# Decay tables and rotary tables moved into the ring of result tiles, seven prepared weights in both layers, and a planner fed with other durations

## The chip, the cores and the metric

One core of a Trainium2 chip runs the whole program. The metric is the device time of one execution in microseconds (us); the profile is of one further execution. TensorE is PE in the profile, VectorE DVE, ScalarE ACT, GpSimd POOL, SyncE SP.

## The reference

Two requests (`x_prompt`, `x_sample`; 512 rows of 1024 each) go through the same two layers and a last RMSNorm, all in float32:

```
layer 1:  x += DiffAttention(RMSNorm(x))   q, k: 16 half-heads of 128; v: 8 heads of 256; rotary on q and k;
          p = softmax(q k'), a = p[first half-head] - lam * p[second]; o = a v; RMSNorm per head;
          o * silu(gate) @ w_out
layer 2:  x += BidirRetention(RMSNorm(x))  q, k: 8 heads of 128 with another rotation; v: 8 heads of 256;
          forward and backward retention with decay exp(-|i-j| * exp(decay)) per head and direction;
          RMSNorm per head; o * silu(gate) @ w_out
y = RMSNorm(x) * final_norm_g
```

Each layer has one input projection (1024 to 8192 columns in layer 1, 1024 to 6144 in layer 2: q, k, v and gate) and one output projection (2048 to 1024).

## The kernel before, in words

**Arithmetic.** Every float32 operand is split in a rounded high part and the rest (`hi_of`, a cast on ACT, L462; `lo_of`, a subtraction on DVE, L465), and each product is three matmuls on these parts (`PASSES`). The two projections also use a seven-product scheme (Strassen's kind): seven products P1 to P7 in place of eight, over the two halves of the columns and of the depth, at the price of sums of weights (`combine`, DVE, L601) and of results (`sums`, DVE, L714).

**A unit** is 256 columns of an input projection. A "pair" unit (q, k, gate) multiplies with the weights stationary: one product is 12 matmuls of 128x512 (`pair_product`, L637). A "wide" unit (v) has 4 times 12 matmuls of 128x256 per product (L685). For a product `prep` loads the raw weights (512 KB each, ring `raw` of 4), sums them where needed (ring `st` of 3) and splits them into the ring `ws` of prepared weights. A pair product takes one place of `ws`, a wide one two. `projections` prepares ahead as far as the ring holds: `WS_BUFS = [7, 6]`, seven places in the second layer (first number), six in the first. The seventh place of layer 1, `ws6`, holds the second request's scaled rotary tables (`ts`, L1026) instead.

**Results** leave the PSUM banks as copies (ring `c`, ACT, L706) and as sums in the ring `e` of eight tiles of 512 columns (`e_t`). For q and k `rot_done` turns them by the tables and `store` splits them into a tile of the ring `os` (three tiles of 1024 columns) and writes that to HBM with two DMAs (`qk<-os`). For v `v_done` splits straight into `os` and writes (`v<-os`). For the gate `gate_done` works in place in the `e` tile and writes that tile (`g<-e`). A place of a ring is free when the last user of its former tile is done, a DMA out of it included: of a q or k unit's four `os` tiles the fourth takes the place of the first, and waits for the first one's store to land.

**Decay tables.** `decay_table(h)` makes, once per head and between the units of the second projection, a 128x896 table of decay factors: it loads distances from HBM (`dist_in`, 448 KB) into one `os` tile, computes the middle 128 columns on DVE (L1487, L1489, L1491), takes three exponentials on ACT (L1492, L1494, L1496) and writes the table to HBM (`f_d[h]`). The retention stage reads it back.

**The stages** by the profile's time: start 0 to 45 us, first input projection to 640, attention with the output projection of layer 1 woven in to 1045, second input projection to 1500, retention with the output projection of layer 2 to the end.

**What sets the order.** All engines are in program order, written out ahead of the run by `Plan`. Each call of `pe`, `act`, `dve`, `pool`, `dma` records one operation with its engine, an assumed duration (`pe(2.79, ...)`, or for ACT and DVE a base and a slope times the number of elements passed, as in `dve(S, ...)` with S = 512), and the tiles that it reads and writes. `arrange` then takes, engine by engine, the ready operation that is due first, counting from these assumed durations, and `issue` keeps the best of three such arrangements. So a changed duration or ring changes the order on all engines, even where no instruction is added. SP has one queue: a DMA that waits for its data or its place holds all DMAs behind it.

## Time and profile before

| | |
|---|---|
| three runs | 1833.98, 1838.55, 1843.78 us (median 1838.55) |
| the profiled execution | 1848.99 us, its span on the core 1847.2 us |
| PE busy | 1796.4 us, 97% of the span, 10100 matmuls |
| DVE, ACT, POOL busy | 1480.1, 1034.9, 227.9 us |
| DMA | 393.85 MB, mean 213 GB/s |

PE counts as busy from a matmul's start to its modelled end, and matmuls overlap; what is not busy, 50.8 us, is time in which PE had nothing in work. In a table of stages each row has the stage, its length, the busy time of each engine with the number of instructions, the granted PE clock (1.00 is full) and the DMA share. In a list of waits each row names who waited for whom, then the total in us, the times, and the longest. In a chain each row is the start, the length and what ran.

### The profile page before, as it was taken

Reading aid. Unit: us, or ns where it says so; the run is one execution under the profiler, and the core shown is the slowest. Engines: PE = TensorE matmul, PEld = TensorE weight load, DVE = VectorE, ACT = ScalarE, POOL = GpSimd, SP = SyncE. Lnnn points to the kernel's source line nnn. Section 1 sums busy time; section 2 is a strip of 40 time slices with the busy share of each in tenths; the row PEclk is TensorE's granted clock in tenths of the full one; section 3 lists DMA queues with packets and bytes.
Section 4 is the critical chain, followed back from the end, with each engine's and each line's share of the span. In section 5 each row is a group of like instructions: output and inputs, shape, how many; then the busy total and the mean of one; then the engine's idle time right before and its main releaser. Section 6 shows DMA issues by size and latency. Waiting matters only on the chain.

```text
span 1847.2 us, 28202 instructions
## 1 busy us (share of the span) xinstructions
PE 1796.4 (97%) x10100; PEld 1545.2 (84%) x10100; DVE 1480.1 (80%) x2597; ACT 1034.9 (56%) x2154; POOL 227.9 (12%) x372
## 2 busy tenths in 40 slices
PE   7999999999999999999999999999999999999997
PEld 6987988988988878888888788978888897888876
DVE  8988778778777998888888898686767758777677
ACT  7644434344434587777777774444443547666663
POOL 2000000000000033333333100000000000111111
PEclk9999999999999999999999999999999999999999
DMA  7557956975544678888785467787784568989883
GB/s 264 194 151 218 264 170 193 269 214 157 172 143 137 230 263 254 250 228 244 231 248 180 138 197 205 229 240 203 216 234 143 165 227 295 248 241 263 235 242 137
DMA packets 195116, 393.85 MB, mean 213 GB/s; under 512 B 16032, under 2 KB 75040, under 8 KB 194848
## 3 DMA queue, kind: packets, MB, share of 16 engines
q1 hardware_dynamic: 172160, 350.02, 56.3%
q0 software_dynamic: 22528, 41.95, 14.5%
q8 instruction: 79, 1.29, 0.3%
q14 instruction: 61, 0.50, 0.1%
q10 hardware_dynamic: 288, 0.08, 0.0%
HBM read 254.10 MB, written 175.64 MB: 233 GB/s over the span
## 4 chain that ended last, share of the span: by engine, by line
PE 74%; DMA 9%; DVE 8%; ACT 4%; issue 3%; POOL 1%; SPq 0%; DVEq 0%; POOLq 0%; ACTq 0%
PE bank L637 34%; PE bank L685 16%; PE bank L1373 10%; PE bank L1564 4%; PE bank L1256 3%; PE bank L1205 3%; DMA b<-w1P 2%; DMA qk<-os 2%; PE bank L1546 2%; DVE b L465 1%; PE bank L893 1%; DMA raw<-in_da_w_in_dram 1%; PE bank L1241 1%; DMA b<-in_da_w_out_dram 1%; DMA b<-w0P 1%
## 5 line engine op out<-in xcount | busy, mean ns | idle before, releaser
L637 PE MATMUL bank<-arena,ws 128*128 128x512 f32 x2202 | 529.2, 394 | 14.1 <-ACT ws L462 7.2
L637 PEld LDWEIGHTS bank<-arena,ws 128*128 128x128 f32 x2202 | 413.8, 189 | 107.0 <-ACT c L706 9.4
L637 PE MATMUL bank<-b,ws 128*128 128x512 f32 x1170 | 287.9, 393 | 2.8 <-DVE e L714 1.8
L637 PEld LDWEIGHTS bank<-b,ws 128*128 128x128 f32 x1170 | 219.2, 188 | 52.0 <-DVE e L714 3.1
L1373 PE MATMUL bank<-b,b 128*128 128x512 f32 x800 | 212.6, 398 | 3.3 <-DVE b L1398 2.1
L685 PE MATMUL bank<-ws,arena 128*128 128x256 f32 x1728 | 208.3, 279 | 0.0
L685 PEld LDWEIGHTS bank<-ws,arena 128*128 128x128 f32 x1728 | 204.6, 189 | 1.4 <-DVE e L786 0.2
L465 DVE TENSOR_TENSOR ws<-st,ws 128x512 fp32r<-128x512 f32 (+1 forms) x188 | 145.6, 778 | 68.8 <-ACT ws L462 58.5
L462 ACT CAST ws<-st 128x512 fp32r<-128x512 f32 (+1 forms) x188 | 129.5, 693 | 125.9 <-PE bank L637 71.2
L706 ACT COPY c<-bank 128x512 f32<-128x512 f32 x165 | 96.0, 582 | 177.1 <-PE bank L637 137.2
L1373 PEld LDWEIGHTS bank<-b,b 128*128 128x128 f32 x800 | 145.6, 188 | 35.5 <-DVE b L1427 3.0
L465 DVE TENSOR_TENSOR b<-b,b 128x512 fp32r<-128x512 f32 (+2 forms) x204 | 137.7, 687 | 20.9 <-ACT b L462 19.7
L462 ACT CAST b<-b 128x512 fp32r<-128x512 f32 (+2 forms) x204 | 124.1, 623 | 49.1 <-DVE b L1550 15.9
L465 DVE TENSOR_TENSOR ws<-raw,ws 128x512 fp32r<-128x512 f32 (+1 forms) x143 | 110.4, 777 | 46.9 <-ACT ws L462 40.4
L714 DVE TENSOR_TENSOR e<-bank,c 128x512 f32<-128x512 f32 x165 | 113.5, 688 | 31.6 <-PE bank L637 23.8
L953 POOL DMA_DIRECT2D x<-b x96 | 87.1, 953 | 369.6 <-DVE b L1398 243.2
L462 ACT CAST ws<-raw 128x512 fp32r<-128x512 f32 (+1 forms) x143 | 98.9, 698 | 49.4 <-PE bank L637 25.1
L685 PE MATMUL bank<-ws,b 128*128 128x256 f32 x960 | 120.6, 281 | 2.9 <-ACT ws L462 2.9
L685 PEld LDWEIGHTS bank<-ws,b 128*128 128x128 f32 x960 | 116.7, 191 | 4.0 <-ACT ws L462 3.3
L1256 PE MATMUL bank<-arena 128*128 128x256 f32 x768 | 104.1, 285 | 0.6 <-DVE b L1316 0.6
L1221 ACT ACTIVATE b<-bank,nm 128x512 f32<-128x512 f32 x128 | 87.8, 688 | 29.4 <-DVE nm L1213 28.9
L1205 PE MATMUL bank<-arena 128*128 128x512 f32 x384 | 102.2, 399 | 2.0 <-ACT b L1221 1.9
(180 smaller groups left out, 2809.1 us busy)
## 6 DMA issues: line engine op xcount, KB each, us to landing
qk<-os SPq DMA_DIRECT2D x192, 256.0 KB, 4.1
arena<-qk SPq DMA_DIRECT2D x80, 512.0 KB, 7.2
raw<-in_da_w_in_dram SPq DMA_DIRECT2D x64, 512.0 KB, 5.2
v<-os SPq DMA_DIRECT2D x60, 512.0 KB, 5.1
arena<-v SPq DMA_DIRECT2D x48, 512.0 KB, 5.7
x<-b POOLq DMA_DIRECT2D x96, 256.0 KB, 6.6
raw<-in_ret_w_in_dram SPq DMA_DIRECT2D x48, 512.0 KB, 5.3
g<-e SPq DMA_DIRECT2D x49, 256.0 KB, 5.0
```

The costliest lines, as they stand in the source:

```text
L462: act(n, lambda: nc.scalar.copy(dst(), src()), r, w)
L465: dve(n, lambda: nc.vector.tensor_tensor(dst(), src(), hi().bitcast(F32), op=ALU.subtract), r, w)
L637: nc.tensor.matmul(ps.t, a[u][0]()[:, k, :], bt[k][:, v, :], start=(opens and k == 0 and i == 0), stop=(k == 3 and i == 2), skip_group_che ...
L685: nc.tensor.matmul(ps[:, (t % 2) * 256:(t % 2) * 256 + 256], bt[k][:, v, t * P:(t + 1) * P], a[u][0]()[:, k, :], start=(opens and t % 2 == ...
L706: act(S, lambda c=c, ps=ps: nc.scalar.copy(c.t, ps.t), [ps], [c])
L714: dve(S, lambda e=e, ps=ps, c=c: nc.vector.tensor_tensor(e.t, ps.t, c.t, op=ALU.add), [ps, c], [e])
L953: plan.op("POOL", 1.0, lambda: nc.gpsimd.dma_start(out(), in_(), accum_op=ALU.add), r, w, lands=5.5, kb=kb, hold=hold)
L1205: nc.tensor.matmul(s.t, q[:, u, t * P:(t + 1) * P], k[:, v, :], start=(n == 0), stop=(n == 2))
L1221: act(840, lambda j=j, s=s, m=m: nc.scalar.activation(p[:, j, :], s.t, AF.Exp, bias=m.t, accum_out=sm[:, j:j + 1]), [s, m], [(p, j), (sm, j)])
L1256: nc.tensor.matmul(o[:, 0:256], aT[:, a, j * P:(j + 1) * P], v[b][:, j, :], start=(n == 0), stop=(n == 11))
L1373: nc.tensor.matmul(ps.t, pick(A[i], u), (hi, lo)[v][:, i, :], start=(opens and n == 0), stop=(n == 5), skip_group_check=True)
L1564: nc.tensor.matmul(o[:, 0:256], a_[j][:, u, t * P:(t + 1) * P], v_[v][:, j, :], start=(n == 0), stop=(n == 11))
```

## The change

1. **Decay tables in two pieces in the ring `e`.** `decay_table` takes two `e` tiles in place of one `os` tile: columns 0 to 383 in one, 384 to 895 in the other, each with its own load and its own store. The arithmetic is the same. That is two loads and two stores per head for one of each: 16 DMAs more.
2. **The second request's rotary tables** lie in `e6` and `e7` during the first projection, and no longer in `ws6`. While `layer_of[0]` is 0 the ring of results is "E", with six places on e0 to e5; from layer 2 on it is `e` with eight.
3. **`WS_BUFS = [7, 7]`**: with `ws6` free, seven prepared weights in layer 1 too.
4. **Other durations in the plan**: a pair product 2.755 for 2.79, a quarter of a wide product 1.365 for 1.43, three score matmuls 0.69 for 0.70, the 12 matmuls of attention times v 1.37 for 1.44, the six of the output projection 1.38 for 1.39; scalar_tensor_tensor on DVE with 60 elements more at five places; the v split 375 (ACT) and 316 (DVE) elements for 256.

```diff
-WS_BUFS = [7, 6]
+WS_BUFS = [7, 7]
...
     def e_t(name="e"):
-        return work("e", [P, S], 8, name=name)
+        if layer_of[0]:
+            return work("e", [P, S], 8, name=name)
+        return Buf(plan, "E", 6, lambda i: view(wk, "e", i, S, [P, S]), lambda i: where(f"e{i}"))
...
-            dve(S, lambda: nc.vector.scalar_tensor_tensor(
+            dve(S + 60, lambda: nc.vector.scalar_tensor_tensor(
...
-            pe(2.79, fn, [q[1] for q in a] + bt, [ps])
+            pe(2.755, fn, [q[1] for q in a] + bt, [ps])
...
-                pe(1.43, lambda ps=ps, t=t: wide(ps, t), reads, [ps])
+                pe(1.365, lambda ps=ps, t=t: wide(ps, t), reads, [ps])
...
-    ts = place("ws6", [P, 2, S])
-    tab[1] = tuple(((lambda i=i: ts[:, i, :]), (ts, i)) for i in range(2))
+    tab[1] = tuple(((lambda t=t: t.t), t) for t in (place(n, [P, S], F32, S) for n in ("e6", "e7")))
...
-        t = os_t(F32, "F")
-        Fd = t.t.rearrange("p a s -> p (a s)")
-        dma(lambda: Fd[:, 0:896], lambda: dist_in, [], [t], 448)
+        a, b = e_t("F"), e_t("F")
+        dma(lambda: a[:, 0:384], lambda: dist_in[:, 0:384], [], [a], 192)
+        dma(lambda: b.t, lambda: dist_in[:, 384:896], [], [b], 256)
...
-        dma(lambda: f_d[h][:], lambda: Fd[:, 0:896], [t], [f_d[h]], 448)
-
+        dma(lambda: f_d[h][:, 0:384], lambda: a[:, 0:384], [a], [(f_d[h], 0)], 192)
+        dma(lambda: f_d[h][:, 384:896], lambda: b.t, [b], [(f_d[h], 1)], 256)
+
+    layer_of[0] = 1
```

In the rows below a name's first number is its place in the ring (`os_2` is the third `os` place); the second only tells tiles of one program apart. Lines of the changed program stand 3 or 4 higher than those of the one before.

**First place: the fifth decay table (`f4`), near 1230 us.** SP's queue before: the load of the distances goes into the place `os_2`, whose two stores stand just ahead of it, and stands between the two stores of the unit's third `os` tile.

```order
L458 DMA qk1021_159<-os_1_237 64x1024 x2
L458 DMA qk1021_159<-os_2_221 64x1024 x2
L458 DMA qk1020_155<-os_0_226 64x1024
L458 DMA os_2_221<-in_dist_dram 128x896
L458 DMA qk1020_155<-os_0_226 64x1024
L458 DMA raw_3_9587<-in_ret_w_in_dram 128x4x256
L458 DMA qk1020_155<-os_1_237 64x1024 x2
L458 DMA f4_193<-os_2_221 128x896
L458 DMA raw_0_9554<-in_ret_w_in_dram 128x4x256
```

SP's queue in the changed program at the same table:

```order
L462 DMA qk1021_159<-os_1_814 64x1024 x2
L462 DMA qk1020_155<-os_2_872 64x1024 x2
L462 DMA qk1020_155<-os_0_767 64x1024
L462 DMA e_7_10016<-in_dist_dram 128x384
L462 DMA e_0_9750<-in_dist_dram 128x512
L462 DMA qk1020_155<-os_0_767 64x1024
L462 DMA f4_193<-e_7_10016 128x384
L462 DMA raw_0_9554<-in_ret_w_in_dram 128x4x256
L462 DMA f4_193<-e_0_9750 128x512
```

The two loads go to `e` places and stand behind the first store of the unit's last `os` tile, where the one load stood behind the first store of its third tile; between them and the table's first store stands one DMA, where three stores of q and a weight load stood.

DVE at the same table before (`small` is where the middle columns are computed, `lr` the decay rates):

```order
L465 TENSOR_TENSOR os_1_237<-e_5_9803,os_1_237 128x512
L601 TENSOR_TENSOR st_0_9666<-raw_0_9554 128x512
L465 TENSOR_TENSOR ws_0_9635<-st_1_9672,ws_0_9635 128x512
L1487 TENSOR_SCALAR small_75<-os_2_221,lr_0_9882 128x128
L1489 TENSOR_SCALAR small_75<-os_2_221,lr_0_9882 128x128
L1491 TENSOR_TENSOR small_75<-small_75 128x128
L714 TENSOR_TENSOR e_1_10011<-bank_3_404,c_0_341 128x512
L739 SCALAR_TENSOR_TENSOR m_1_9559<-e_1_10011,cos_0_369 128x512
L465 TENSOR_TENSOR ws_1_9664<-st_2_9685,ws_1_9664 128x512
L739 SCALAR_TENSOR_TENSOR e_1_10011<-e_1_10011,sin_0_399 128x512
L714 TENSOR_TENSOR e_2_10047<-bank_1_317,c_3_9683 128x512
```

DVE in the changed program:

```order
L469 TENSOR_TENSOR os_0_767<-e_2_9802,os_0_767 128x512
L718 TENSOR_TENSOR e_6_9995<-bank_3_400,c_0_338 128x512
L469 TENSOR_TENSOR ws_1_9673<-st_2_9676,ws_1_9673 128x512
L743 SCALAR_TENSOR_TENSOR m_1_9559<-e_6_9995,cos_0_395 128x512
L743 SCALAR_TENSOR_TENSOR e_6_9995<-e_6_9995,sin_0_398 128x512
L718 TENSOR_TENSOR e_1_9760<-bank_1_314,c_3_9688 128x512
L469 TENSOR_TENSOR ws_2_9684<-st_0_9664,ws_2_9684 128x512
L743 SCALAR_TENSOR_TENSOR m_2_9528<-e_1_9760,sin_0_398 128x512
L1490 TENSOR_SCALAR small_75<-e_0_9750,lr_0_9883 128x128
L1492 TENSOR_SCALAR small_75<-e_0_9750,lr_0_9883 128x128
L774 TENSOR_TENSOR m_1_9559<-m_1_9559,m_2_9528 128x512
L1494 TENSOR_TENSOR small_75<-small_75 128x128
```

The two sums that empty the banks 3 and 1 stood behind the table's first instruction and now stand ahead of it.

**Second place: the ring of six, near 50 us.** DVE before, from the gate's last step on `e_4` to that on `e_0`; the first sum of the wide unit goes into `e_6`:

```order
L789 SCALAR_TENSOR_TENSOR e_4_610<-c_0_341,e_4_610 128x512
L789 SCALAR_TENSOR_TENSOR e_5_627<-c_1_361,e_5_627 128x512
L465 TENSOR_TENSOR ws_1_283<-st_2_566,ws_0_275 128x1024
L1106 TENSOR_TENSOR b_3_252<-m_3_330,b_3_252 128x512
L714 TENSOR_TENSOR e_6_719<-bank_5_592,c_2_584 128x512
L465 TENSOR_TENSOR b_18_651<-b_2_246,b_18_651 128x512
L465 TENSOR_TENSOR b_19_654<-b_2_246,b_19_654 128x512
L465 TENSOR_TENSOR b_20_669<-b_3_252,b_20_669 128x512
L465 TENSOR_TENSOR b_21_721<-b_3_252,b_21_721 128x512
L789 SCALAR_TENSOR_TENSOR e_0_545<-e_1_580,e_0_545 128x512
```

DVE in the changed program, from the gate's last step on `e_0` to the same sum:

```order
L793 SCALAR_TENSOR_TENSOR e_0_539<-e_1_574,e_0_539 128x512
L605 TENSOR_TENSOR st_0_491<-raw_2_260,raw_0_251 128x1024
L469 TENSOR_TENSOR ws_6_421<-st_2_572,ws_5_419 128x1024
L790 TENSOR_TENSOR e_4_624<-e_4_624,small_75 128x512
L790 TENSOR_TENSOR e_5_641<-e_5_641,small_75 128x512
L1109 TENSOR_TENSOR b_4_249<-m_2_310,b_4_249 128x512
L793 SCALAR_TENSOR_TENSOR e_4_624<-c_0_338,e_4_624 128x512
L793 SCALAR_TENSOR_TENSOR e_5_641<-c_1_358,e_5_641 128x512
L1109 TENSOR_TENSOR b_4_249<-m_3_327,b_4_249 128x512
L718 TENSOR_TENSOR e_0_539<-bank_5_581,c_2_578 128x512
```

The sum now goes into `e_0`, so the gate's last step, its scaling on ACT and its store to HBM have moved ahead of it, with eight DVE instructions between.

**Third place: PE's first turns of row norms, near 30 us.** PE before, from the fifth product on (L1060 is one 128x128 transpose that spreads row norms):

```order
L637 MATMUL bank_3_404<-arena_76,ws_0_275 128x512 x12
L637 MATMUL bank_4_426<-arena_76,ws_1_283 128x512 x12
L1060 MATMUL bank_7_450<-ident_0_250,b_8_385 128x128
L637 MATMUL bank_3_404<-arena_76,ws_2_286 128x512 x12
L1060 MATMUL bank_7_450<-ident_0_250,b_9_389 128x128
L1060 MATMUL bank_7_450<-ident_0_250,b_10_392 128x128
L637 MATMUL bank_4_426<-arena_76,ws_3_304 128x512 x12
L1060 MATMUL bank_7_450<-ident_0_250,b_11_395 128x128
```

PE in the changed program:

```order
L641 MATMUL bank_3_400<-arena_76,ws_0_272 128x512 x12
L641 MATMUL bank_4_423<-arena_76,ws_1_280 128x512 x12
L641 MATMUL bank_3_400<-arena_76,ws_2_283 128x512 x12
L1063 MATMUL bank_7_473<-ident_0_247,b_9_380 128x128
L1063 MATMUL bank_7_473<-ident_0_247,b_10_384 128x128
L641 MATMUL bank_4_423<-arena_76,ws_3_301 128x512 x12
L1063 MATMUL bank_7_473<-ident_0_247,b_11_387 128x128
L1063 MATMUL bank_7_473<-ident_0_247,b_12_391 128x128
```

The first transpose stands one product later. Over the whole program PE's order of products, scores and transposes differs at 50 of 1265 places, by a step or two each.

More of the change, by code (lines that the diff above doesn't have):

```diff
@@ L1080, in times @@
         def times(out, kg, x, less, r, w):
-            dve(S, lambda: nc.vector.scalar_tensor_tensor(
+            dve(S + 60, lambda: nc.vector.scalar_tensor_tensor(
                 out(), x(), gain(0, kg), less(), op0=ALU.mult, op1=ALU.subtract), r + [gcol], w)
@@ L1205, in fn @@
                     nc.tensor.matmul(s.t, q[:, u, t * P:(t + 1) * P], k[:, v, :], start=(n == 0), stop=(n == 2))
-            pe(0.7, fn, [q, k], [s])
+            pe(0.69, fn, [q, k], [s])
             st[i]['s'].append(s)
@@ L1258, in fn @@
                     n += 1
-        pe(1.44, fn, [aT, *v], [(o, 0)])
+        pe(1.37, fn, [aT, *v], [(o, 0)])
         rc = st[i]['rc']
@@ L1375, in fn @@
                         n += 1
-            pe(1.39, fn, [*A, hi, lo], [ps])
+            pe(1.38, fn, [*A, hi, lo], [ps])
             if p < LASTP:
@@ L1487, in decay_table @@
         dve(P, lambda: nc.vector.tensor_scalar(
-            mid.t, Fd[:, 384:512], 0.0, lr[:, 0, h:h + 1], op0=ALU.max, op1=ALU.mult), [t, lr], [mid])
+            mid.t, b[:, 0:P], 0.0, lr[:, 0, h:h + 1], op0=ALU.max, op1=ALU.mult), [b, lr], [mid])
         dve(P, lambda: nc.vector.tensor_scalar(
-            mid2.t, Fd[:, 384:512], 0.0, lr[:, 1, h:h + 1], op0=ALU.min, op1=ALU.mult), [t, lr], [mid2])
+            mid2.t, b[:, 0:P], 0.0, lr[:, 1, h:h + 1], op0=ALU.min, op1=ALU.mult), [b, lr], [mid2])
         dve(P, lambda: nc.vector.tensor_tensor(mid.t, mid.t, mid2.t, op=ALU.add), [mid, mid2], [mid])
-        act(384, lambda: nc.scalar.activation(Fd[:, 0:384], Fd[:, 0:384], AF.Exp, scale=lr[:, 1, h:h + 1]),
-            [lr], [t])
-        act(384, lambda: nc.scalar.activation(Fd[:, 512:896], Fd[:, 512:896], AF.Exp, scale=lr[:, 0, h:h + 1]),
-            [lr], [t])
-        act(P, lambda: nc.scalar.activation(Fd[:, 384:512], mid.t, AF.Exp), [mid], [t])
-        dma(lambda: f_d[h][:], lambda: Fd[:, 0:896], [t], [f_d[h]], 448)
+        act(384, lambda: nc.scalar.activation(a[:, 0:384], a[:, 0:384], AF.Exp, scale=lr[:, 1, h:h + 1]), [lr], [a])
+        act(384, lambda: nc.scalar.activation(b[:, P:S], b[:, P:S], AF.Exp, scale=lr[:, 0, h:h + 1]), [lr], [b])
+        act(P, lambda: nc.scalar.activation(b[:, 0:P], mid.t, AF.Exp), [mid], [b])
+        dma(lambda: f_d[h][:, 0:384], lambda: a[:, 0:384], [a], [(f_d[h], 0)], 192)
+        dma(lambda: f_d[h][:, 384:896], lambda: b.t, [b], [(f_d[h], 1)], 256)
+    layer_of[0] = 1
     tab2 = [load_tab(rot_tab)] * NG
@@ L1546, in fn @@
                 nc.tensor.matmul(s.t, k[:, u, j * P:(j + 1) * P], q[:, v, :], start=(i == 0), stop=(i == 2))
-        pe(0.7, fn, [q, k], [s])
+        pe(0.69, fn, [q, k], [s])
         t1 = turns("rt", [P, S])
@@ L1566, in fn @@
                     n += 1
-        pe(1.44, fn, [*a_, *v_], [(o, 0)])
+        pe(1.37, fn, [*a_, *v_], [(o, 0)])
         os_[b, t] = o
```

9 lines of the change are left out of this document (5 added, 4 removed).

## The prediction

> **What bounds the kernel now.** I read the page's first part, then the stages, then who PE waits for, then the stage in which the change acts.
>
> ```profile
> PE 1796.4 (97%) x10100; PEld 1545.2 (84%) x10100; DVE 1480.1 (80%) x2597; ACT 1034.9 (56%) x2154; POOL 227.9 (12%) x372
> ```
> ```profile
> 0.00:45.00 45.00, 35.51 (x180) 28.98 (x181) 35.96 (x60) 34.73 (x57) 10.15 (x20) 1.00 0.77 270
> 45.00:640.00 595.00, 589.40 (x3191) 507.73 (x3190) 488.70 (x783) 268.07 (x474) 15.92 (x16) 1.00 0.64 191
> 640.00:1045.00 405.00, 396.39 (x2292) 336.48 (x2290) 355.51 (x715) 298.69 (x738) 136.61 (x256) 1.00 0.77 237
> 1045.00:1500.00 455.00, 445.81 (x2537) 389.94 (x2538) 338.37 (x521) 221.85 (x370) 16.09 (x17) 1.00 0.67 196
> ```
> ```profile
> PE bank L637 <- ACT c L706: 7.9, 6, 3.0
> ...
> PE bank L685 <- ACT ws L462: 2.9, 1, 2.9
> PE bank L1124 <- ACT b L447: 2.8, 1, 2.8
> PE bank L1060 <- DVE b L1058: 2.2, 3, 1.0
> ```
>
> PE is the bound, and the change takes no matmul away. So it can only win where PE stands idle: 9.5 us in the start (45.00 less 35.51), 5.6 in the first projection, 8.6 in attention, 9.2 in the second projection. The reader is to see how small these are beside 1847 us: a change of the order alone is worth some tens of us at most, and the two stages that this one aims at hold 14.8 together. What PE waits for there is seldom weights (`ws`, once, 2.9 us), mostly the copies that empty a bank (`c`, L706): ACT and DVE stand in order behind something else.
>
> **Decay tables out of the `os` ring.** What they stand behind in the second projection:
>
> ```profile
> DVE small L1487 <- DMA os<-in_dist_dram: 11.4, 3, 4.7
> DVE st L601 <- DMA raw<-in_ret_w_in_dram: 11.2, 5, 4.2
> ```
> ```profile
> SPq L458 <- ACT os L1496: 16.0, 7, 4.4
> SPq L458 <- DMA qk<-os: 14.0, 3, 6.4
> ```
> ```profile
> 1222.76 8.13 DMA qk<-os
> ```
> ```profile
> 1230.96 3.64 DMA os<-in_dist_dram
> ```
> ```profile
> 1229.81 0.69 DVE L601 TENSOR_TENSOR st<-raw 128x512 f32<-128x512 f32 x1
> 1230.41 0.69 DVE L465 TENSOR_TENSOR ws<-st,ws 128x512 fp32r<-128x512 f32 x1
> 1234.62 0.28 DVE L1487 TENSOR_SCALAR small<-os,lr 128x128 f32<-128x128 f32 x1 [3.52 <-DMA os<-in_dist_dram]
> ```
> ```profile
> 1238.62 1.65 PE L637 MATMUL bank<-b,ws 128*128 128x512 f32 x6 [1.31 <-DVE e L714]
> ```
> ```profile
> 1252.91 3.02 PE L637 MATMUL bank<-arena,ws 128*128 128x512 f32 x12 [3.01 <-ACT c L706]
> ```
> ```profile
> 1163.14 1.65 PE L637 MATMUL bank<-b,ws 128*128 128x512 f32 x6 [0.26 <-DVE e L714]
> ```
>
> Read downwards, this is the fifth table. The load of the distances wants the `os` place that a q store still reads; that store takes 8.13 us, SP stands until it has landed, the load takes 3.64 more, and DVE, at L1487, stands for 3.52 us with the bank sum L714 behind it. PE then idles 1.31 us. All that DVE does for the unit, its `os` tiles too, is 3.5 us late, so the fourth `os` tile waits later for the first one's store, ACT stands there, and PE idles 3.01 us at 1252.91. Two tables of eight do it in small (4.7 us, and 11.4 - 4.7 - 3.5 = 3.2): there PE loses 0.26 us each, as in the last row. The other five tables stop DVE nowhere.
>
> In the changed order the loads go into `e` places, whose last users are older by two units or more, so SP no longer stands for a q store. What is left at L1490: behind the unit's last `os` split DVE has seven instructions of 0.60 us (the distance of the two rows ahead of L1487), 4.2 us. On SP in that time stand one store and the two loads:
>
> ```profile
> 1225.71 0.45 SPq L458 DMA_DIRECT2D qk<-os  x1
> 1230.96 0.35 SPq L458 DMA_DIRECT2D os<-in_dist_dram  x1
> ```
> ```profile
> os<-in_dist_dram SPq DMA_DIRECT2D x8, 448.0 KB, 4.2
> ```
>
> That is 0.45 + 0.35 + a landing of 3.64 (this table) to 4.2 us (the median of eight): 4.4 to 5.0. DVE waits some 0.2 to 0.8 us instead of 3.52, and the two bank sums stand ahead of the wait, no longer behind it. I take the worse, 3.52 - 0.8 = 2.7 us, and it all returns, since PE's two gaps there hold 1.31 + 3.01 = 4.3 us. With 0.26 twice: **-3.2 us**. Bounds: 0, if the fourth tile's wait stays as late as it is, and -4.8 (4.3 + 0.5).
>
> What stays is the fourth `os` tile behind the first one's store: without the table in between, the fourth tile is still three places on.
>
> **Sixteen more DMAs** of half the size are hidden: an issue is 0.35 us and SP stands for others most of the time. If that cover were gone they would cost 16 x 0.35 = 5.6 us. In the changed rows the table's first store stands almost directly behind its loads, so SP now stands there for the load and ACT's exponentials. Behind it is a weight load; this is a rival below. In the sum: 0, up to +5.6.
>
> **Tables of rotation in e6 and e7** cost nothing by themselves, the same two loads and the same reads. The price is the ring of six. Later on, result tiles are in use for less than six turns, by the trace's times of their users; near 50 us, with the gates' tiles, they are not. There the sum of the wide unit goes into `e_0`, and must wait for `e_0`'s scaling and its store:
>
> ```profile
> 49.33 1.22 DVE L465 TENSOR_TENSOR ws<-st,ws 128x1024 fp32r<-128x1024 f32 x1
> 50.46 0.69 DVE L1106 TENSOR_TENSOR b<-m,b 128x512 f32<-128x512 f32 x1
> ```
> ```profile
> 54.79 0.72 ACT L791 ACTIVATE e<-e,gcol 128x512 f32<-128x512 f32 x1
> ```
> ```profile
> DMA to landing us min/median/max: 2.5/3.7/6.5
> ```
>
> The eight DVE instructions between take 2 x 1.13 (1024 columns, the distance of the first two rows) + 6 x 0.60 = 5.9 us. The way through the store is 0.72 + 2.5, 3.7 or 6.5 us (the gate stores of 40 to 110 us), with some 0.1 between engines: 3.3, 4.5 or 7.3. So DVE waits 0 there, 1.4 at worst; a second such place right behind it (`e_2`, some 4.8 us of DVE between) 0, 2.5 at worst. I take **+0.5 us**, with 0 and +3.9 as ends.
>
> **Seven prepared weights in layer 1** give PE one product more in hand. PE waited for weights once, 2.9 us at 366.48:
>
> ```profile
> 366.48 7.42 PE L685 MATMUL bank<-ws,b 128*128 128x256 f32 x48 [2.85 <-ACT ws L462]
> ```
> ```profile
> 1196.14 5.47 PE bank L685 x48
> ```
> ```profile
> 366.50:371.00 4.50, 4.50 (x25) 4.50 (x26) 3.87 (x9) 0.59 (x2) 0.92 (x1) 0.62 1.07 298
> ...
> 1253.00:1256.00 3.00, 3.00 (x14) 2.47 (x15) 0.63 (x1) 0.95 (x2) 0.00 (x0) 1.00 0.92 196
> ```
>
> The split of the v tiles stands ahead of these weights on ACT and behind a q store, and that order is the same after the change. So I take 0. The end is the whole gap and what follows it: the granted clock was 0.62 behind it, and the 48 matmuls took 7.42 us where such a set takes 5.47 elsewhere, so 2.85 + 1.95 = -4.8. On the other side +1: weights split earlier stand ahead of a bank's copy on ACT.
>
> Behind the equally long gap at 1252.91 the clock stayed at 1.00 (last row), so I add nothing for it. The Trainium skill, "TensorE: Matmul & The Clock Gate", section "What's actually happening", has the clock halve after an idle window of about 3.4 us, and return after as long a busy one, which is 1.7 us lost each time. The trace agrees only in part: both gaps, 2.85 and 3.01 us, are shorter than that window, yet the first cost 1.95 us more and the second nothing. Had the clock fallen at the second too, the page's 1.7 us would make the term of the tables -4.9 in place of -3.2.
>
> **The start.** PE stands at three single transposes:
>
> ```profile
> 27.40 0.33 PE L1060 MATMUL bank<-ident,b 128*128 128x128 f32 x1 [0.91 <-DVE b L1058]
> ...
> 32.07 0.33 PE L1060 MATMUL bank<-ident,b 128*128 128x128 f32 x1 [1.00 <-DVE b L1058]
> ```
>
> The first moves behind a product of 12 matmuls, 2.75 us, so its 0.91 goes; the second was never late for the product ahead of it and now follows the first directly. I take **-1.0 us**, between -2.2 (all three) and 0.
>
> **The other durations** move single steps on ACT, DVE and SP everywhere. They are nearer to the rows in the projections (1.365 against 5.47 / 4 = 1.37) and farther in attention:
>
> ```profile
> 794.41 1.41 PE bank L1256 x12
> ```
>
> 1.41 stands against 1.37 now and 1.44 before, so the plan is out by 0.04 where it was by 0.03. I take 0, and +3 to -3, a third of attention's 8.6 us of PE idle.
>
> **The sum.** -3.2 + 0.5 - 1.0 = -3.7 us, of the profiled execution's 1848.99: 1845.3. That execution is 10.4 us above the median of the runs, 1838.55; against the median the forecast is **1834.9 us**. A measurement of this kernel tells 0.5%, some 9 us, from no change, so this counts as no difference.
>
> **Rivals.** First, more comes: with seven weights and `os` free both projections run through. PE's idle there, 14.8 us, less the 2.8 us at L1124 where the stages meet, 12.0, with 1.95 for the clock and 1.0 in the start: 1838.55 - 15 = 1823.6. For it speaks that most gaps hang on one late DVE or ACT; against it that the q stores of 8 us remain and hold ACT as before.
>
> Second, the wait moves: the tables no longer stop DVE, but the fourth `os` tile does, at the same time, since it waits for a store that HBM traffic makes slow. Then the first term is near 0 and the time 1838. For it speaks the 3.01 us gap, which waits for such a store and not for a table.
>
> Third, slower: SP is the bound of the second projection. The table's first store stands directly behind its loads, and SP stands 4.2 us for the load and 0.6 for an exponential, some 5 us, at each of eight tables, with a weight load behind.
>
> ```profile
> L1492 ACT ACTIVATE os<-os,lr x8: 608/616/621, 1075.8 to 1357.6; 128x384 f32<-128x384 f32 x8
> ```
>
> DVE waited 11.2 us in five such raw loads already. Waits of DVE reach PE at the rate of the tables' own, 4.0 (3.5 and twice 0.26) of 11.4 us, 0.35: 8 x 5 x 0.35 = +14 us, 1852.5. It decides from the point where a weight load lands later than DVE has other work, about 3 us. Against it: before, SP stood 16.0 us for table stores and 14.0 for their places, and the latter goes.
>
> **Chances.** Forecast (gain of 1 to 9 us) 0.42, more comes 0.24, the wait moves 0.19, slower by SP or by the ring of six 0.15. A part of the forecast's upper end, 0.04, is over 0.5% as well. So faster by over 0.5%: 0.28; slower: 0.14, for a small part of the last case stays within; the same: 0.58. The range reaches from the first rival with the durations' 3 us, 1820, to 1849, where the ends of the ring, the DMAs and the durations (3.9 + 5.6 + 3.0) come together less the start's 1.0, +11: some 0.1 is left on either side.
>
> **What would show it.** Right: no row of waits in which L1490 stands over 1 us for a load of the distances; no SP wait for `qk<-os` ahead of one; PE idle in the second projection 6 us, not 9.2; near 50 us no DVE wait for a `g<-e` store. Wrong: SP standing longer in total for the tables' exponentials and DVE longer for raw weights (third rival), DVE idle at the bank sums near 50 us (ring of six), or the gap near 366 gone with no other in its place (first rival).

## The result and the profile after

The changed kernel takes 1829.42 us, the median of six runs (1825.85 to 1833.37); the kernel before, run beside it, 1838.60 (1832.99 to 1843.78). The ratio is 0.9945, with a 95% interval of [0.9921, 0.9969]: 9.2 us less by the medians, 5.7 to 14.5 us by the interval. The forecast had 3.7 us.

The profiled executions stand 17.8 us apart (spans 1847.2 and 1829.5), but the one of before was slower than all runs of that kernel. A second profile of before, taken for the experiments, has a span of 1838.0 (1839.76 us). Every difference by place below is against this second one; what the two profiles of before differ by is the uncertainty of such a number.

The page of the changed kernel, and its stages (same columns as in the prediction):

```profile
PE 1790.0 (98%) x10100; PEld 1545.4 (84%) x10100; DVE 1481.2 (81%) x2598; ACT 1035.7 (57%) x2153; POOL 226.6 (12%) x372
```
```profile
0.00:45.00 45.00, 34.57 (x181) 28.91 (x182) 35.02 (x58) 35.79 (x58) 12.15 (x20) 1.00 0.76 270
45.00:640.00 595.00, 590.87 (x3211) 511.10 (x3210) 495.64 (x793) 271.68 (x478) 15.93 (x16) 1.00 0.65 194
640.00:1045.00 405.00, 395.75 (x2293) 336.43 (x2293) 355.22 (x715) 299.37 (x739) 132.50 (x256) 1.00 0.77 232
1045.00:1500.00 455.00, 455.00 (x2617) 400.43 (x2617) 343.80 (x529) 221.84 (x371) 15.83 (x16) 1.00 0.68 203
```

The last row matters most: in the second projection PE idled 9.2 us before and now not at all. Of the 9.2 us, 2.8 stood right at the stage's start (1047 us, L1124); that gap is now 1.4 us and comes at 1041.7 us, in the row above. The first projection still has 4.1 us of idle, the start 10.4 (9.5 before), attention 9.3 (8.6).

What DVE, ACT and SP wait for in the second projection, 1040 to 1490 us: first ACT in the kernel before, then three answers on the changed one.

```profile
ACT os L462 <- DMA qk<-os: 13.7, 6, 4.4
```
```profile
ACT os L466 <- DMA qk<-os: 3.8, 2, 1.9
```
```profile
DVE st L605 <- DMA raw<-in_ret_w_in_dram: 9.9, 4, 4.0
...
DVE small L1490 <- DMA e<-in_dist_dram: 0.6, 1, 0.6
```
```profile
SPq L462 <- ACT e L1495: 42.8, 7, 13.8
...
SPq L462 <- ACT e L1497: 7.8, 5, 1.9
```

DVE's 11.4 us at the tables are 0.6. ACT's waits for a q store to free an `os` place, 13.7 us (11.1 in the second profile of before), are 3.8. SP now stands 50.6 us (42.8 and 7.8) for the tables' exponentials, and DVE's waits for raw weights have not grown for it (11.2 us before).

The timeline of the fifth table after: SP issues five q stores in a row, then both loads together; DVE reaches L1490 when the distances are there.

```profile
1217.80 8.24 SPq L462 DMA_DIRECT2D qk<-os  x5
...
1226.10 1.27 SPq L462 DMA_DIRECT2D e<-in_dist_dram  x2
...
1230.44 0.28 DVE L1490 TENSOR_SCALAR small<-e,lr 128x128 f32<-128x128 f32 x1
```

What PE still waits for, by the list of its waits over the span, and its two gaps in the first projection by the timeline:

```profile
...
PE bank L897 <- ACT small L891: 3.8, 4, 2.2
PE bank L1208 <- ACT b L1224: 3.3, 3, 2.0
...
PE bank L689 <- DVE e L718: 2.4, 1, 2.4
...
PE bank L689 <- ACT c L710: 1.7, 1, 1.7
PE bank L689 <- DVE e L790: 1.7, 1, 1.7
```
```profile
354.25 5.73 PE L689 MATMUL bank<-ws,b 128*128 128x256 f32 x48 [1.71 <-ACT c L710]
...
365.15 7.31 PE L689 MATMUL bank<-ws,b 128*128 128x256 f32 x48 [2.43 <-DVE e L718]
```

So the gap at 366 us, which the prediction left as it was, is still there in another form: two gaps, 4.1 us together, and slow matmuls behind the second (7.31 us for 48, where 5.73 is the set before). Ahead of the first ACT stands for raw weights:

```profile
351.79 0.62 ACT L466 CAST ws<-raw 128x512 fp32r<-128x512 f32 x1 [9.38 <-DMA raw<-in_da_w_in_dram]
```

### The profile page after: what moved, and what is told of

Read it like the earlier page. It is cut to its first block, busy times and chain, and to the rows that moved or that the text cites. A ratio compares the mean times of both kernels' runs of the same rounds, so it can differ in the third digit from the quotient of the medians.

```text
span 1829.5 us, 28194 instructions
## 1 busy us (share of the span) xinstructions
PE 1790.0 (98%) x10100; PEld 1545.4 (84%) x10100; DVE 1481.2 (81%) x2598; ACT 1035.7 (57%) x2153; POOL 226.6 (12%) x372
## 4 chain that ended last, share of the span: by engine, by line
PE 52%; DMA 4%; DVE 3%; issue 2%; ACT 1%; POOL 1%; DVEq 0%; POOLq 0%; ACTq 0%
PE bank L641 16%; PE bank L1376 12%; PE bank L689 9%; PE bank L1259 4%; PE bank L1208 4%; PE bank L1567 3%; DMA b<-w1P 3%; PE bank L1549 1%; PE bank L897 1%; PE bank L1244 1%; DVE b L469 1%; DVE arena L469 1%; DMA b<-in_da_w_out_dram 0%; DMA b<-w0P 0%; DVE b L1319 0%
```

## The experiments

All kernels of the study, with the parts of the change that each holds (1 the decay tables; 2 the ring of six results with the rotary tables; 3 seven weights in layer 1; 4 the durations). "Before" is the median of the kernel before on the same chip.

| kernel | holds | median (range), us | before | ratio [95%] |
|---|---|---|---|---|
| changed kernel | 1 2 3 4 | 1829.42 (1825.85 to 1833.37) | 1838.60 | 0.9945 [0.9921, 0.9969] |
| tables_alone | 1 | 1829.46 (1824.57 to 1832.53) | 1837.12 | 0.9952 [0.9933, 0.9971] |
| ring_alone | 2 3 | 1825.32 (1821.86 to 1831.42) | 1837.12 | 0.9936 [0.9915, 0.9958] |
| durations_alone | 4 | 1826.68 (1822.29 to 1831.54) | 1837.12 | 0.9947 [0.9928, 0.9966] |
| without_durations | 1 2 3 | 1823.42 (1819.17 to 1825.80) | 1839.80 | 0.9911 [0.9892, 0.9930] |
| without_ring | 1 4 | 1821.10 (1817.46 to 1826.67) | 1839.80 | 0.9904 [0.9881, 0.9927] |
| without_tables | 2 3 4 | 1830.85 (1827.38 to 1833.56) | 1839.80 | 0.9958 [0.9941, 0.9975] |
| copies_apart | 1 2 3 4, copies moved | 1823.00 (1819.66 to 1832.91) | 1839.80 | 0.9917 [0.9891, 0.9944] |
| copies_only | copies moved | 1834.87 (1831.18 to 1842.31) | 1838.58 | 0.9983 [0.9965, 1.0001] |
| six_results | 2 | 1833.80 (1826.96 to 1839.16) | 1838.58 | 0.9968 [0.9950, 0.9986] |
| two_cures | 1 4, copies moved | 1823.64 (1821.39 to 1827.95) | 1838.58 | 0.9919 [0.9889, 0.9948] |

And where PE won or lost the time in the profiled execution of each. PE does the same 10100 matmuls in nearly the same order in all of them, so I took from each trace the time at which PE starts its n-th matmul. A column is the time from one such matmul to another, less the same in the second profile of before (us; negative is faster; the times in the heads are those of before).

| kernel | no. 600 to 800 (113 to 160 us) | 1800 to 2600 (339 to 482) | 3200 to 5200 (597 to 955) | 5600 to 8200 (1029 to 1495) | span |
|---|---|---|---|---|---|
| before, first profile | +1.1 | +3.0 | -1.6 | +4.1 | +9.2 |
| changed kernel | -1.7 | +2.7 | -1.6 | -5.5 | -8.5 |
| tables_alone | -0.5 | +0.3 | -0.7 | -9.3 | -12.9 |
| ring_alone | -1.7 | -3.6 | -0.8 | +3.4 | -8.4 |
| durations_alone | -0.9 | -3.6 | -4.0 | -6.2 | -17.6 |
| without_durations | -1.7 | -3.6 | -1.7 | -6.6 | -15.5 |
| without_ring | -1.0 | -3.6 | -3.5 | -10.2 | -22.3 |
| without_tables | -1.7 | -0.4 | -3.9 | +0.4 | -8.0 |
| copies_apart | +0.7 | -3.6 | -1.9 | -7.7 | -10.8 |
| copies_only | -0.6 | -3.6 | -0.9 | -0.7 | -6.7 |
| six_results | -1.7 | -2.5 | -0.3 | -0.5 | -5.5 |
| two_cures | -1.7 | -3.6 | -2.5 | -9.5 | -15.6 |

Each row is one execution. Two executions of the kernel before differ by up to 4.1 us in a column, so less than that in a single cell proves nothing; a value that comes back, as -3.6 does, is a place without any gap. The profiled execution was the fastest of its six for durations_alone and without_ring and the second slowest for ring_alone and copies_apart, which shifts the last column. And a column holds more than idle time: between no. 5600 and 8200 tables_alone has 5.8 us less idle than before and takes 3.6 us less for the same matmuls, the changed kernel has 6.6 us less idle and takes 1.1 us more for them. What makes the matmuls faster or slower there was not followed.

### First set: before once more, and each part alone

before_again is the unchanged kernel, for a second profile. It gave 1839.76 us.

> The kernel before once more, for a second profile. The changed kernel's profile is 17.75 us shorter than the first profile of before, its runs only 9.2 us in the median. If half of the 17.75 us was one slow execution, this span is 1833 to 1840 us and some of the PE gaps of the first profile (1.0 and 0.9 at 145 and 149 us, 3.0 at 1253, 1.5 at 1352, 2.0 at 1535) are smaller; if every gap belongs to the program, the same gaps stand at the same products, within 0.5 us each.

Its span is in the expected range. The gaps stand at the same products, but not within 0.5 us of their size: the one at 1253 us is 1.02 us here where it was 3.01, one of the two near 145 us is gone, and the one near 366 us is half as long:

```profile
364.74 5.69 PE L685 MATMUL bank<-ws,b 128*128 128x256 f32 x48 [1.44 <-ACT ws L462]
```

tables_alone, part 1 on the kernel before:

```diff
-        t = os_t(F32, "F")
+        a, b = e_t("F"), e_t("F")
```

> Before with the decay tables in two pieces in the ring of result tiles, nothing else. Theory (the tables' waits in the os ring are what the second projection lost): 5 to 8 us faster, ratio 0.9957 to 0.9973, with PE idle in the second projection down from 9.2 us to under 3 and the rest as before. Rival (the order from the other durations did it): within 2 us of before.

ring_alone, parts 2 and 3:

```diff
-WS_BUFS = [7, 6]
+WS_BUFS = [7, 7]
...
+        return Buf(plan, "E", 6, lambda i: view(wk, "e", i, S, [P, S]), lambda i: where(f"e{i}"))
```

> Before with the second rotary tables in e6 and e7, six result tiles in the first projection and seven prepared weights, nothing else. Theory: 2 to 3 us faster, from the two gaps near 145 and 149 us that the changed kernel no longer has; the second projection as before. Rival (the ring does nothing): within 1 us; rival (the ring of six costs): 2 us slower, with DVE waits for a gate's store near 50 us.

durations_alone, part 4 (all its numbers; two of them here):

```diff
-            pe(2.79, fn, [q[1] for q in a] + bt, [ps])
+            pe(2.755, fn, [q[1] for q in a] + bt, [ps])
...
-                pe(1.43, lambda ps=ps, t=t: wide(ps, t), reads, [ps])
+                pe(1.365, lambda ps=ps, t=t: wide(ps, t), reads, [ps])
```

> Before with the planner's other durations alone. Theory: within 2 us of before, with the waits of L1487 for the load of the distances still at 8 us or more in total. Rival: 4 us faster or more, with PE idle in the second projection under 5 us though the tables are still in the os ring.

tables_alone came out as its theory had it, its ratio a little below the range. The two others did not: ring_alone gained 11.8 us where 2 to 3 were expected, durations_alone 10.4 where its theory allowed 2, and of its rival both signs came (over 4 us, and under 5 us of idle in the second projection with the tables still in `os`).

Each part alone gains what all gain together: 7.7, 11.8 and 10.4 us, 29.9 in sum, against 9.2. So the parts do not add up, and a sum over parts, as the prediction made it, cannot be the right book-keeping. The table by place fits better: PE gains at two large places, and each part alone cures one of them. tables_alone has the second projection but keeps the gap near 366 us. ring_alone has the first projection (-3.6 is what is left when there is no gap at all) but not the second; durations_alone has the first wholly and the second in part. PE between 1047 and 1490 us, 443 us long, in the second profile of before, in tables_alone, ring_alone and durations_alone (length, then PE busy):

```profile
1047.00:1490.00 443.00, 437.70 (x2491) 381.08 (x2489) 335.52 (x519) 217.64 (x364) 15.85 (x16) 1.00 0.68 200
```
```profile
1047.00:1490.00 443.00, 442.49 (x2564) 388.04 (x2563) 337.04 (x520) 219.17 (x367) 15.85 (x16) 1.00 0.68 204
```
```profile
1047.00:1490.00 443.00, 436.74 (x2494) 381.71 (x2494) 328.02 (x505) 213.32 (x354) 15.84 (x16) 1.00 0.68 202
```
```profile
1047.00:1490.00 443.00, 439.64 (x2552) 385.57 (x2551) 332.06 (x512) 214.33 (x356) 15.85 (x16) 1.00 0.69 206
```

Idle 5.3 us before, 0.5 with the tables alone, 6.3 with the ring alone, 3.4 with the durations alone.

What cures the first place? The weights of the wide unit near 366 us are loaded some 25 us earlier, and six copies of 512 KB from HBM to HBM (`w0P` from `weight_sums`, rows of `x`), all triggered by one q tile, can stand ahead of them in SP's queue. SP's order in the changed kernel (the first number counts the lines of the listing):

```
143 L462 DMA w0P53_217<-in_da_w_out_dram 256x1x512
144 L462 DMA w0P63_218<-in_da_w_out_dram 256x1x512
145 L462 DMA x12_203<-in_x_sample_dram 16x8192
146 L462 DMA w0P43_219<-in_da_w_out_dram 256x1x512
147 L462 DMA w0P73_220<-in_da_w_out_dram 256x1x512
148 L462 DMA x13_204<-in_x_sample_dram 16x8192
149 L462 DMA raw_0_251<-in_da_w_in_dram 128x4x256
150 L462 DMA qk0131_108<-os_2_872 64x1024 x2
151 L462 DMA qk0131_108<-os_0_767 64x1024 x2
152 L462 DMA raw_1_255<-in_da_w_in_dram 128x4x256
```

and in ring_alone:

```
143 L462 DMA w0P53_217<-in_da_w_out_dram 256x1x512
144 L462 DMA w0P63_218<-in_da_w_out_dram 256x1x512
145 L462 DMA x12_203<-in_x_sample_dram 16x8192
146 L462 DMA raw_0_254<-in_da_w_in_dram 128x4x256
147 L462 DMA qk0131_108<-os_2_221 64x1024 x2
148 L462 DMA raw_1_258<-in_da_w_in_dram 128x4x256
```

Six copies ahead against three; in ring_alone the other three go out at 443 us. The DMA view of 330 to 348 us has the two weight loads issued there; the last column is the median time to landing. Before, the changed kernel, ring_alone and durations_alone:

```profile
raw<-in_da_w_in_dram SPq DMA_DIRECT2D x2, 512.0 KB, 13.4
```
```profile
raw<-in_da_w_in_dram SPq DMA_DIRECT2D x2, 512.0 KB, 13.2
```
```profile
raw<-in_da_w_in_dram SPq DMA_DIRECT2D x2, 512.0 KB, 7.9
```
```profile
raw<-in_da_w_in_dram SPq DMA_DIRECT2D x2, 512.0 KB, 10.8
```

durations_alone has the six copies ahead too, but its loads land at 346.5 and 350.0 us, those of the changed kernel at 351.8 and 355.7. There the second load also stands behind two pairs of q stores, for which SP needs 8.49 us, and is issued at 345.1 us, in durations_alone at 339.8. From this came the theory for the second set: the order that the planner happens to make decides at two places, and each place is cured or not. Its rival: any other order gives some 10 us.

### Second set: one part undone, and the copies moved

without_durations, the changed kernel with the old numbers:

```diff
-            pe(2.755, fn, [q[1] for q in a] + bt, [ps])
+            pe(2.79, fn, [q[1] for q in a] + bt, [ps])
...
```

> Tables and ring (with seven weights) as in the changed kernel, the plan's durations as before. Theory of places: the parts act at two places, and each place is cured or not by the order that comes out. First projection: SP has three of the six 512 KB copies from HBM to HBM ahead of the wide unit's weight loads, as with the ring alone, so the loads land in about 8 us, PE has no gap over 1 us between 345 and 380 us, and the 48 matmuls there take 5.5 us each set. Second projection: no DVE wait over 1 us for the distances, ACT under 5 us for q stores, PE idle under 1.5 us between 1047 and 1490 us. Both cured: the changed kernel's 1829.4 less 7.8 us (its lead at the 2600th matmul is 3.2 us, that of the ring alone 11.0): about 1821.6 us. Rival, any other order gives the same 10 us (each part alone took 8 to 12 us): 1825 to 1830, with the gap at 366 us or another of its size somewhere.

without_ring:

```diff
-WS_BUFS = [7, 7]
+WS_BUFS = [7, 6]
...
-        if layer_of[0]:
-            return work("e", [P, S], 8, name=name)
-        return Buf(plan, "E", 6, lambda i: view(wk, "e", i, S, [P, S]), lambda i: where(f"e{i}"))
+        return work("e", [P, S], 8, name=name)
```

> Tables and durations as in the changed kernel; the results have eight places and the weights of layer 1 six, as before. Theory of places: SP's queue in the first projection is that of the durations alone (six copies ahead of the weight loads, but these issued some us earlier against PE's need), so the loads land in 10 to 11.5 us and PE has no gap over 1 us near 366 us; second projection as in the changed kernel, PE idle there under 1.5 us. The changed kernel's 1829.4 less 6.5 us (lead at the 2600th matmul 9.7 against 3.2 us): about 1823 us. Rival, any other order gives the same: 1825 to 1830.

without_tables:

```diff
-        a, b = e_t("F"), e_t("F")
+        t = os_t(F32, "F")
```

> Ring, seven weights and durations as in the changed kernel; the decay tables stay in the tiles os, one load and one store each. Theory of places: SP's queue in the first projection is that of the changed kernel (six copies ahead of the weight loads), so a gap of 2 to 5 us and slow matmuls behind it come back near 366 us. Second projection: DVE waits 6 to 12 us for the distances, ACT about 11 us for q stores, PE idle 3 to 6 us between 1047 and 1490 us. So neither place is cured: the changed kernel's 1829.4 plus 3 to 5 us, about 1833 us, against 1837 before. Rival, any other order gives the same 10 us: 1825 to 1829.

copies_apart, the changed kernel with another trigger for half of the copies:

```diff
-        weight_sums(0, n // 2, n % 2, qk_d[0, 0, n // 2, 0])
+        weight_sums(0, n // 2, n % 2, qk_d[0, n % 2, n // 2, 0])
...
-        dma(lambda g=g, t=t: x_d[g, t][:], lambda g=g, t=t: xs[g][0, t * P:(t + 1) * P, :], [qk_d[0, 0, n // 2, 0]],
+        dma(lambda g=g, t=t: x_d[g, t][:], lambda g=g, t=t: xs[g][0, t * P:(t + 1) * P, :], [qk_d[0, n % 2, n // 2, 0]],
```

> The changed kernel with one edit: half of the copies from HBM to HBM of layer 1 (weights' sums, rows of x) are triggered by the other request's k tile, so that none of the six stands ahead of the wide unit's weight loads near 340 us; the six go out together near 420 us instead. If the copies ahead of them make the weight loads late, these land in about 8 us in place of 15.8 and 10.5, and PE's gaps of 1.7 and 2.4 us near 354 and 366 us with the slow matmuls behind them go: the changed kernel's 1829.4 less 6 to 8 us, about 1822 us, unless a gap near 420 us takes their place. Rival, the loads are late for another reason (the copies only stand beside them): ACT still waits 9 us for raw weights there and the time stays at 1829.

The two pairs that hold the tables gain more than all three parts: 16.4 us (without_durations) and 18.7 (without_ring) against 9.2, though the intervals of both still overlap with that of the changed kernel, that of without_ring by 0.0006 only. Both medians came within 2 us of the theory of places, as did that of copies_apart, and all three lie below what their rivals gave. The loads of without_durations and copies_apart land in

```profile
raw<-in_da_w_in_dram SPq DMA_DIRECT2D x2, 512.0 KB, 7.8
```
```profile
raw<-in_da_w_in_dram SPq DMA_DIRECT2D x2, 512.0 KB, 8.7
```

in copies_apart with none of the six copies ahead of them. The stretch from 345 to 380 us (length, then PE busy) of copies_apart has no idle time, where the changed kernel has 4.1 us:

```profile
345.00:380.00 35.00, 35.00 (x245) 32.34 (x244) 23.10 (x42) 15.93 (x32) 0.00 (x0) 1.00 0.76 236
```
```profile
345.00:380.00 35.00, 30.87 (x209) 28.51 (x208) 21.96 (x40) 15.15 (x30) 3.92 (x4) 0.95 1.01 288
```

The six copies now go out at 446 to 450 us, and copies_apart lost 2.4 us between no. 2600 and 3200 (482 to 597 us), the only kernel with a loss there; whether the copies did it was not followed.

without_tables lost the second projection as expected (PE idle 5.9 us there, DVE 10.2 us at the distances, ACT 14.3 at the q stores, row below) and kept a gap of 2.96 us at 364 us. Yet at 1830.85 us it lies between the theory's 1833 and its rival's 1825 to 1829, within the noise of the changed kernel, and 9.0 us below the kernel before with neither place cured. By its places 3.9 us of that are in attention. So the two places explain why the pairs are faster, but not all that a kernel gains.

```profile
1047.00:1490.00 443.00, 437.14 (x2504) 381.77 (x2503) 329.82 (x509) 214.71 (x357) 15.84 (x16) 1.00 0.68 202
```

### Third set: the copies alone, the ring of six alone, and both cures

copies_only is the kernel before with the edit of copies_apart and nothing else.

> The kernel before, with nothing of the change, and one edit: half of the copies from HBM to HBM of layer 1 are triggered by the other request's k tile. In SP's queue three of the six then stand ahead of the wide unit's weight loads near 340 us, the other three go out near 420 us. Theory of places: the loads land in about 8 us in place of 13, PE's gap of 2.85 us at 366 us and the slow matmuls behind it (1.95 us) go, and the second projection stays as it was (DVE waits 9 to 12 us for the distances, PE idle 5 to 7 us between 1047 and 1490 us): 1839.8 less 5 us, about 1835 us, and at most as good as the ring alone, 1825 to 1830. Rival, the copies are not what makes the loads late: 1838 to 1841, with the gap at 366 us still there.

six_results is ring_alone without the seventh weight:

```diff
-WS_BUFS = [7, 7]
+WS_BUFS = [7, 6]
```

> The ring part without its seventh weight: results on six places in layer 1, the rotation tables in e6 and e7, six prepared weights as before; decay tables and durations as before. SP's queue near 340 us has all six copies ahead of the weight loads, as before. Theory of places: nothing cures the first projection (a gap of 2 to 5 us with what follows near 366 us) nor the second (PE idle 5 to 7 us between 1047 and 1490 us), so within 4 us of before: 1836 to 1841 us, and a stop of DVE near 50 us for a gate's store of 1.4 us at most. Rival, the ring of six itself is what gave the ring part its 11 us: about 1828 us.

two_cures is without_ring with the edit of copies_apart.

> Decay tables in two pieces and the plan's durations as in the changed kernel, results on eight places and six weights in layer 1 as before, and the copies triggered apart (three of six ahead of the weight loads). Theory of places: both places are cured already without the copies' edit, so it adds at most what a landing of 11 us against 8 us still costs: 1818 to 1823 us, no gap over 1 us between 345 and 380 us, PE idle under 1.5 us between 1047 and 1490 us. Rival, the cures add up: 1821 less 6 us, about 1815 us.

copies_only gives 1834.87 us, the theory's 1835, though its interval just reaches 1. The weight loads land in

```profile
raw<-in_da_w_in_dram SPq DMA_DIRECT2D x2, 512.0 KB, 5.9
```

and PE runs through from 345 to 380 us:

```profile
345.00:380.00 35.00, 35.00 (x241) 32.21 (x240) 24.14 (x42) 15.88 (x31) 2.88 (x3) 1.00 0.85 241
```

So the copies make the loads late: when they are moved, in the kernel before and in the changed one, the gap goes. (The planner moves other steps with them: the loads of copies_only are also issued 5 us earlier, at 336.4 us.) In six_results SP has six copies ahead again, the loads take 14.4 us and a gap stays, but of 0.49 us only. Its loads were issued at 338.1 and 338.7 us where the kernel before had 341.7 and 343.6, so how early the load is issued seems to count beside what stands ahead of it. So with the durations as before it is the seventh weight, not the ring of six, that changes the order of the copies. six_results came out 2 us under its expected range, 4.8 us under the kernel before, so the ring of six moves something too, but not the 11.8 us of ring_alone. two_cures, 0.6 us above its expected range, adds nothing to without_ring: where the first place has no gap, moving the copies gains nothing, as the theory had it.

The best of the study is without_ring, decay tables and durations without the ring: 1821.10 us, 0.9904 [0.9881, 0.9927]. The four kernels with both places cured lie between 1821.1 and 1823.6 and are not told apart.

## Why the prediction was right or wrong

The direction was right and the time lies in the range. The forecast called the change no difference; the ratio of 0.9945 stands just past its bound of 0.5%, and the interval leaves out 1. The size was wrong, 3.7 us against 9.2. By the places, of the 8.5 us between the profiles: second projection -5.5, the gaps near 145 us -1.7, attention -1.6, the place near 366 us +2.7 (the first profile of before has +3.0 there), the rest -2.4. The ends that make up the slow bound add up to +11.5, 1850 us, and not to 1849; nothing hangs on it.

- **Decay tables, -3.2 forecast.** This is the mis-sized term: PE's idle between 1047 and 1490 us fell from 5.3 us (7.2 in the first profile) to 0, and the place gained 5.5; by the runs part 1 alone takes off 7.7 us. The step that failed is "What stays is the fourth `os` tile behind the first one's store". It did not stay: ACT's wait for it fell from 13.7 us (11.1 in the second profile) to 3.8. In all five kernels with part 1 profiled beside the changed one it is 3.8 to 4.1, in all seven profiles without part 1 that have the tables in `os` 7.4 to 14.3. A table in the ring held a place from its load to the landing of its store, so the q tiles found two places for four. That this is the reason is argued from the order; a ring of four `os` tiles with the tables left in it wasn't tried. The forecast counted the wait that it saw at the tables and not the ring's other users.
- **Loads, waits, order at L1490**: 0.2 to 0.8 us forecast, 0.6 measured; no row over 1 us, as said.
- **Sixteen more DMAs, 0**: right. The third rival's cause came in full, SP standing 50.6 us where 40 were forecast, and its effect didn't: DVE's wait for raw weights is 9.9 us, below the 11.2 before. In the five other kernels with part 1 it is 9.1 to 16.4 us (6.3 to 14.4 in those without), yet PE idles under 1 us there between 1047 and 1490 us. So neither SP's standing nor these waits reach PE at the rate of 0.35, which was taken from the tables' waits.
- **The ring of six, +0.5**: DVE has no wait for a gate's store near 50 us. Right at the lower end. The gaps of some 1 us each at 145 and 149 us, which the forecast has no term for, are gone. They are gone in five of the six kernels with the ring of six and in one of the five without it; copies_apart, with it, lost 0.7 us there, and two_cures, without it, has no gap. So the ring helps there, but by the order that comes with it.
- **Seven weights, 0 between -4.8 and +1**: The step that failed is "that order is the same after the change". It looked at ACT and not at SP. With the durations as before, the seventh weight moves three copies behind the weight loads and is worth the whole gap (-3.6 in ring_alone, 0 idle); with the durations beside it the copies stand ahead again, and the place is 2.7 us worse than in the second profile of before, 0.3 better than in the first. So 0 was near, but by luck: it came of two parts that undo each other at this place and not of an order that stays.
- **The start, -1.0**: wrong, about 0. One transpose still waits (0.53 us), and a gap behind a step of the gate on DVE (L790) is new:

```profile
30.43 0.33 PE L1063 MATMUL bank<-ident,b 128*128 128x128 f32 x1 [0.53 <-DVE b L1061]
...
38.44 4.38 PE L689 MATMUL bank<-ws,arena 128*128 128x256 f32 x36 [1.65 <-DVE e L790]
```

- **Durations, 0 within 3**: in the six profiles with part 4, attention gains 1.6 to 4.0 us, in the other five 0.3 to 1.7, and 1.6 in the first profile of before. So about -2 there on the average, inside the bounds and hardly outside the noise. But the same numbers alone gave 10.4 us, mostly by what they did to the order in both projections, which the forecast did not see.
- **The first rival, "more comes", 1823.6**, is what happens once both projections run through: 1821.1 to 1823.6 in four kernels. The changed kernel got one half of it. The second rival, "the wait moves" to the fourth `os` tile, is refuted by the 3.8 us.

Open: ring_alone is 11.8 us faster than before by its runs and 8.4 by its profile, and copies_only, with the same first projection, only 3.7; the 3 to 5 us between them at small places were not followed up. Open too is why without_tables gains 9.0 us with neither place cured, and why the planner puts the copies ahead with parts 3 and 4 together and not with part 3 alone.

## What to carry to other kernels

Where a planner makes the order, the parts of a change need not add up: book the time by place in the program (when does the bound engine start its n-th instruction), and try all pairs; here, by the medians, each pair with the tables beat the three together. Profile the unchanged kernel twice: here its gaps differed by up to 2 us. A gap on the bound engine is to be followed to the queue in which the late load stood, and to what stood ahead of it: weight loads behind three of the bulk copies took 6 to 8 us, behind six 10 to 14. A tile that is moved out of a ring can relieve every user of that ring, not only the wait at which it was seen.

## What the runs showed of the hardware

A load's time to landing went with the bulk copies that stood ahead of it on the same queue. The two 512 KB weight loads took 5.9 to 7.9 us (median of the two) in the four kernels with three copies ahead, 10.4 to 14.4 us in the eight profiles with six, and 8.7 us in copies_apart with none. In the kernel before the six copies land one after the other from 341.6 to 353.2 us, and the two loads behind them at 355.3 and 356.7. Whether it is the order in the queue that holds the loads or the traffic as such, no run tells apart: from 335 to 355 us the DMA engines moved 314 GB/s in the kernel before and 272 in copies_only.

The clock after a gap does not follow the gap's length. The place near 364 us in tables_alone and without_tables, PE's 48 matmuls and then the stretch from 366 to 370 us (third number from the end is the granted clock):

```profile
364.60 7.30 PE L685 MATMUL bank<-ws,b 128*128 128x256 f32 x48 [2.09 <-ACT ws L462]
```
```profile
366.00:370.00 4.00, 4.00 (x26) 4.00 (x26) 3.32 (x7) 1.79 (x4) 0.92 (x1) 0.67 1.02 353
```
```profile
364.32 5.71 PE L689 MATMUL bank<-ws,b 128*128 128x256 f32 x48 [2.96 <-DVE e L718]
```
```profile
366.00:370.00 4.00, 4.00 (x37) 4.00 (x36) 3.50 (x8) 2.10 (x5) 0.92 (x1) 1.00 1.03 348
```

After 2.09 us of idle the granted clock fell and the set took 7.30 us; after 2.96 us it stayed at 1.00 and the set took 5.71. The changed kernel had 2.43 us and 7.31. The 0.67 is a mean: the clock is 0.50 until 368.64 us and 1.00 from there.

Where the gap lies makes the difference. Apart from the first and last microseconds of a trace, the clock in the 13 traces falls to 0.50 for 3.41 us at a time (once for twice that), and the falls of one trace start a whole number of 3.41 us apart, 199 and 144 of them in the first profile of before. On this grid the gap of 2.09 us lies whole in one stretch, 361.82 to 365.23 us, and the fall is the next one. The gap of 2.96 us is split, 1.89 us into the stretch to 363.25 us and 1.07 into the one behind it, and no fall follows. Over the 13 traces a fall follows each of the 15 stretches with 2.0 us of idle or more, and none begins behind a stretch with 1.7 or less; in between both happen.

The Trainium skill, "TensorE: Matmul & The Clock Gate", section "What's actually happening", has the clock halve after an idle window of about 3.4 us, and this window runs freely. The length of 3.41 us, and a grid that no gap shifts, agree with it; that the window has to be idle throughout does not, since 2.0 us of it were enough.
